# Seven products of half blocks for a SwiGLU's gate and up projections: a float32 decoder block on one core

## The chip, the core and the metric

The kernel runs on one core of a Trainium2 chip. The core has a matrix engine (PE, whose weight loads are shown apart as PEld), a vector engine (DVE), a scalar engine (ACT), a general engine (POOL) and a queue engine (SP) that here only issues transfers. They run side by side, each takes its own instructions in order, and they wait for one another by semaphores. The metric is the device time of one execution in microseconds (us); lower is better.

## The reference

One decoder layer for 512 positions of 1024 features: a half-step feed-forward, a mixing part with causal attention and a gated chunk mixer, and a second half-step feed-forward. Only the two feed-forwards are changed:

```python
D_MODEL = 1024; SEQ = 512; D_FF = 2816

def swiglu(h, w_gate, w_up, w_down):
    return (jax.nn.silu(h @ w_gate) * (h @ w_up)) @ w_down

x = x + 0.5 * swiglu(rms_norm(x, ffn1_norm[l]), ffn1_w_gate[l], ffn1_w_up[l], ffn1_w_down[l])
...
x = x + m @ w_out[l]
x = x + 0.5 * swiglu(rms_norm(x, ffn2_norm[l]), ffn2_w_gate[l], ffn2_w_up[l], ffn2_w_down[l])
```

## The kernel before

Activations lie feature-major: eight tiles of 128 features by 512 positions. A float32 product is made of three PE products of a rounded type: each operand is split into a rounded part (hi, a copy on ACT) and the rest (lo = source - hi, a subtraction on DVE), and `mm3` adds hi x hi, hi x lo and lo x hi in one bank of PSUM. PSUM has eight banks of 128x512, four under the name acc and four under att.

`ffn` is called twice (pools ff1 and ff2). It loops over 22 blocks `f` of 128 hidden features. For each, `dense` loads a 128x1024 chunk of gate weights and one of up weights, splits each, and runs 8 x 3 products for each chunk, 512 columns wide. `evacuate(f)` runs one block behind: DVE multiplies both banks by the row scale `r_bc` (L225, L228), ACT takes the SiLU, DVE multiplies (L229), and the result is split into `a_hi[f]`, `a_lo[f]`. After the last block comes the down projection: for each of 8 output tiles `j`, all 22 blocks are added in one bank, and `finish` adds half of it to the residual tile.

`prepare` names work put in after a block: in the first feed-forward the sum of squares and the scale after block 0 and the constants of the mixing part after block 8, in the second the scale after block 1. The raw weights have two buffers and the split weights three, so the queue loads and the splits run about two chunks ahead of PE. In the mixing part, `add_out` ends the stage before the second feed-forward: eight units of 24 products, each followed by the residual sum, `normed_input` (xg_hi on ACT, xg_lo on DVE) and `add_squares`.

A scheduler fixes the order of each engine's instructions when the program is built; the code's order is where it starts from.

Of the kernel before, what the change touches and what calls it, by code (L numbers as in the profile page):

```python
# [13 lines left out]
F32 = mybir.dt.float32  # L14
F32R = mybir.dt.float32r
# [5 lines left out]
P = 128  # L21
# [23 lines left out]
WARM = 8  # L45

# [10 lines left out]
def decoder_block(  # L57
# [85 lines left out]
    ones = const.tile([P, P], F32, name="ones")  # L143
# [3 lines left out]
    nc.vector.memset(ones, 1.0)  # L147
    nc.vector.memset(eps_col, NORM_EPS)
    ones_r = const.tile([P, P], F32R, name="ones_r")
    nc.vector.tensor_copy(ones_r, ones)  # L150
# [3 lines left out]
    for _ in range(WARM):  # L154
        nc.tensor.matmul(ps[:, :P], lhsT=ones, rhs=ones, start=True, stop=True)
# [18 lines left out]
    sq_sum = keep.tile([P, T], F32, name="sq_sum")  # L174
    x1_dram = [tc.dram_tile([P, T], F32, name=f"x1_dram{j}") for j in range(KD)]
# [28 lines left out]
    def dense(srcs, load=None):  # L204

        cuts = 1 if load is None else 4
        w = [chunk(src, cuts=cuts) for src in srcs]
        ps = [any_bank() for _ in srcs]
        for k in range(KD):
            s = slice(k * P, (k + 1) * P)  # L210
            if load is not None:
                load(k)
                if k % 2 == 0:
                    for c in w:
                        c[2](k // 2)
            for c, o in zip(w, ps):
                mm3(o, c[0][:, s], c[1][:, s], xg_hi[k], xg_lo[k], k == 0, k == KD - 1)
        return ps

    def ffn(pool, gu, dn, finish, load, prepare):  # L220
        a_hi, a_lo = [], []

        def evacuate(f, gate, up):
            g = scratch()
            nc.vector.tensor_tensor(g, gate, r_bc, op=ALU.mult)  # L225
            nc.scalar.activation(g, g, AF.Silu)
            u = scratch()
            nc.vector.tensor_tensor(u, up, r_bc, op=ALU.mult)  # L228
            nc.vector.tensor_tensor(u, u, g, op=ALU.mult)  # L229
            hi = pool.tile([P, T], F32R, name=f"a_hi{f}")  # L230
            lo = pool.tile([P, T], F32R, name=f"a_lo{f}")
            split(hi, lo, u)
            a_hi.append(hi)
            a_lo.append(lo)

        waiting = deque()
        for f in range(NF):
            if f == 0:
                banks = dense([gu[f, 0], gu[f, 1]], load)
            else:  # L240
                banks = dense([gu[f, 0]]) + dense([gu[f, 1]])
            waiting.append((f, *banks))
            if f in prepare:
                prepare[f]()
            if f > 0:
                evacuate(*waiting.popleft())
        evacuate(*waiting.popleft())
        for j in range(KD):
            ps = any_bank()
            for f0 in range(0, NF, 8):  # L250
                n = min(8, NF - f0)
                hi, lo = chunk(dn[j, :, f0 * P : (f0 + n) * P], n * P)
                for i in range(n):
                    s = slice(i * P, (i + 1) * P)
                    f = f0 + i
                    mm3(ps, hi[:, s], lo[:, s], a_hi[f], a_lo[f], f == 0, f == NF - 1)
            finish(j, ps)
# [73 lines left out]
    with tc.tile_pool(name="ff1", bufs=1) as ff1:  # L331
# [15 lines left out]
        def finish1(j, ps):  # L347
            nc.vector.scalar_tensor_tensor(xt[j], ps, 0.5, xt[j], op0=ALU.mult, op1=ALU.add)
            normed_input(j, xt[j], 1)
            add_squares(j, xt[j])  # L350
            nc.gpsimd.dma_start(out=x1_dram[j], in_=xt[j])

        ffn(ff1, gu1, dn1, finish1, load1, {0: prepare1, 8: constants1})


    x1 = []
# [541 lines left out]
```

## Time and profile before

| | |
|---|---|
| median of 3 runs | 1212.06 us (1212.02 to 1213.16) |
| the profiled execution's own time | 1214.09 us |
| its span, first to last instruction | 1212.4 us |
| PE busy | 99% of the span, 5322 products |
| DVE busy, ACT busy | 53%, 41% |
| granted PE clock, mean | 0.999 of full speed |
| bytes moved | 115.60 MB, 95 GB/s |

The page gives for each engine its busy time; the chain that ended last names, from the end backwards, what each step waited for. Three stages follow one another: the first feed-forward to about 415 us, the mixing part to about 838 us, and the second feed-forward. A share over the whole span mixes them, so the rows further down are read stage by stage.

### The profile page before, as it was taken

Reading aid. Unit: us, or ns where it says so; the run is one execution under the profiler, and the core shown is the slowest. Engines: PE = TensorE matmul, PEld = TensorE weight load, DVE = VectorE, ACT = ScalarE, POOL = GpSimd, SP = SyncE. Lnnn points to the kernel's source line nnn. Section 1 sums busy time; section 2 is a strip of 40 time slices with the busy share of each in tenths; the row PEclk is TensorE's granted clock in tenths of the full one; section 3 lists DMA queues with packets and bytes.
Section 4 is the critical chain, followed back from the end, with each engine's and each line's share of the span. In section 5 each row is a group of like instructions: output and inputs, shape, how many; then the busy total and the mean of one; then the engine's idle time right before and its main releaser. Section 6 shows DMA issues by size and latency. Waiting matters only on the chain.

```text
span 1212.4 us, 13634 instructions
## 1 busy us (share of the span) xinstructions
PE 1200.9 (99%) x5322; PEld 970.0 (80%) x5322; DVE 639.3 (53%) x1110; ACT 495.2 (41%) x756; POOL 24.1 (2%) x50
## 2 busy tenths in 40 slices
PE   8999999999999999999999999999999999999998
PEld 6888888888888888888878787888888888888886
DVE  5646444433333767876778876554543444442221
ACT  6324232222222554557587966233422323221110
POOL 0000000000000100000000000000000000000000
PEclk9999999999999999999999999999999999999999
DMA  5332322223333322222212124322323222233330
GB/s 176 104 109 87 98 94 93 98 78 113 113 113 122 127 91 87 70 87 71 70 53 87 35 74 153 104 87 87 104 87 105 87 93 98 90 98 113 113 112 31
DMA packets 34432, 115.60 MB, mean 95 GB/s; under 512 B 4032, under 2 KB 5088, under 8 KB 34368
## 3 DMA queue, kind: packets, MB, share of 16 engines
q1 hardware_dynamic: 32544, 109.07, 27.8%
q0 software_dynamic: 1824, 5.67, 1.5%
q8 instruction: 41, 0.67, 0.2%
q14 instruction: 23, 0.19, 0.0%
HBM read 110.53 MB, written 4.19 MB: 95 GB/s over the span
## 4 chain that ended last, share of the span: by engine, by line
PE 94%; ACT 3%; DVE 2%; DMA 0%; issue 0%; SPq 0%; DVEq 0%; ACTq 0%
PE bank_acc L125 16%; PE bank_acc L123 16%; PE bank_acc L124 16%; PE bank_att L124 10%; PE bank_att L125 10%; PE bank_att L123 10%; PE bank_acc L396 4%; PE bank_acc L395 4%; PE bank_acc L394 4%; PE bank_att L523 1%; PE bank_att L524 1%; PE bank_att L549 1%; DMA x<-in_x 0%; ACT scratch L531 0%; ACT w_hi L137 0%
## 5 line engine op out<-in xcount | busy, mean ns | idle before, releaser
L137 ACT CAST w_hi<-w_raw 128x1024 fp32r<-128x1024 f32 (+2 forms) x210 | 211.2, 1009 | 572.7 <-PE bank_acc L124 270.4
L138 DVE TENSOR_TENSOR w_lo<-w_raw,w_hi 128x1024 fp32r<-128x1024 f32 (+2 forms) x210 | 246.1, 1174 | 176.8 <-ACT w_hi L137 176.3
L123 PE MATMUL bank_acc<-xg_hi,w_hi 128*128 128x512 f32 x512 | 203.8, 398 | 2.5 <-ACT w_hi L137 1.5
L125 PE MATMUL bank_acc<-xg_hi,w_lo 128*128 128x512 f32 x512 | 203.5, 397 | 1.2 <-DVE w_lo L138 1.2
L124 PE MATMUL bank_acc<-xg_lo,w_hi 128*128 128x512 f32 x512 | 203.4, 397 | 0.1
L123 PE MATMUL bank_att<-xg_hi,w_hi 128*128 128x512 f32 x352 | 139.3, 396 | 0.0
L124 PE MATMUL bank_att<-xg_lo,w_hi 128*128 128x512 f32 x352 | 139.2, 396 | 0.0
L125 PE MATMUL bank_att<-xg_hi,w_lo 128*128 128x512 f32 x352 | 139.2, 395 | 0.0
L123 PEld LDWEIGHTS bank_acc<-xg_hi,w_hi 128*128 128x128 f32 x512 | 96.5, 188 | 26.3 <-ACT w_hi L137 2.3
L125 PEld LDWEIGHTS bank_acc<-xg_hi,w_lo 128*128 128x128 f32 x512 | 96.5, 188 | 24.6 <-DVE w_lo L138 1.6
L124 PEld LDWEIGHTS bank_acc<-xg_lo,w_hi 128*128 128x128 f32 x512 | 96.5, 188 | 23.0 <-DVE xg_lo L180 0.5
L228 DVE TENSOR_TENSOR scratch<-bank_att,r_bc 128x512 f32<-128x512 f32 x44 | 30.4, 691 | 132.3 <-PE bank_att L125 132.3
L394 PE MATMUL bank_acc<-w_hi,xg_hi 128*128 128x512 f32 x224 | 89.5, 400 | 0.0
L395 PE MATMUL bank_acc<-w_lo,xg_hi 128*128 128x512 f32 x224 | 88.7, 396 | 0.0
L396 PE MATMUL bank_acc<-w_hi,xg_lo 128*128 128x512 f32 x224 | 88.6, 396 | 0.0
L123 PEld LDWEIGHTS bank_att<-xg_hi,w_hi 128*128 128x128 f32 x352 | 66.1, 188 | 16.2
L125 PEld LDWEIGHTS bank_att<-xg_hi,w_lo 128*128 128x128 f32 x352 | 66.1, 188 | 15.9
L124 PEld LDWEIGHTS bank_att<-xg_lo,w_hi 128*128 128x128 f32 x352 | 66.1, 188 | 15.9
L225 DVE TENSOR_TENSOR scratch<-bank_acc,r_bc 128x512 f32<-128x512 f32 x44 | 30.4, 691 | 88.8 <-PE bank_acc L125 88.7
L125 PE MATMUL bank_att<-a_hi,w_lo 128*128 128x512 f32 x176 | 69.6, 396 | 0.0
L123 PE MATMUL bank_acc<-a_hi,w_hi 128*128 128x512 f32 x176 | 69.6, 396 | 0.0
L124 PE MATMUL bank_acc<-a_lo,w_hi 128*128 128x512 f32 x176 | 69.6, 396 | 0.0
(217 smaller groups left out, 1758.0 us busy)
## 6 DMA issues: line engine op xcount, KB each, us to landing
w_raw<-in_gu SPq DMA_DIRECT2D x86, 512.0 KB, 3.5
w_raw<-in_dn SPq DMA_DIRECT2D x32, 512.0 KB, 3.6
w_raw<-in_w_qk SPq DMA_DIRECT2D x16, 512.0 KB, 3.5
w_raw<-in_dn SPq DMA_DIRECT2D x16, 384.0 KB, 3.1
w_raw<-in_w_v SPq DMA_DIRECT2D x8, 512.0 KB, 3.4
w_raw<-in_w_ga SPq DMA_DIRECT2D x8, 512.0 KB, 3.4
w_raw<-in_w_gb SPq DMA_DIRECT2D x8, 512.0 KB, 3.5
w_raw<-in_w_pb SPq DMA_DIRECT2D x8, 512.0 KB, 3.5
```

What stands on the lines that cost most here:

```text
L123: nc.tensor.matmul(ps, lhsT=lhi, rhs=rhi, start=first, stop=False)
L124: nc.tensor.matmul(ps, lhsT=lhi, rhs=rlo, start=False, stop=False)
L125: nc.tensor.matmul(ps, lhsT=llo, rhs=rhi, start=False, stop=last)
L137: latest["hi"] = nc.scalar.copy(hi, src)
L138: latest["lo"] = nc.vector.tensor_tensor(lo, src, hi, op=ALU.subtract)
L225: nc.vector.tensor_tensor(g, gate, r_bc, op=ALU.mult)
L228: nc.vector.tensor_tensor(u, up, r_bc, op=ALU.mult)
L394: nc.tensor.matmul(banks[t], lhsT=xg_hi[k][:, ts], rhs=hi[:, s], start=k == 0, stop=False)
L395: nc.tensor.matmul(banks[t], lhsT=xg_hi[k][:, ts], rhs=lo[:, s], start=False, stop=False)
L396: nc.tensor.matmul(banks[t], lhsT=xg_lo[k][:, ts], rhs=hi[:, s], start=False, stop=k == KD - 1)
L523: nc.tensor.matmul(s[m], lhsT=qd[m][:, qs], rhs=kd[m][:, :w], start=True, stop=False)
L524: nc.tensor.matmul(s[m], lhsT=ql[m][:, qs], rhs=kd[m][:, :w], start=False, stop=False)
```

## The change

The gate and up projections now go by pairs of blocks (a "quad" `q`: two blocks `f`, gate and up, the lower and the upper half of the 1024 features, and the first and second 256 positions). The eight products of half blocks that the pair needs become seven, by sums of weight halves (`total`, made on DVE for each quad) and sums of activation halves (`half_sums`, made on DVE once for each feed-forward, split into `s_hi`, `s_lo`). Each product has 24 PE instructions 256 columns wide, in place of 512-wide ones. Three of the seven results share the bank `a` in turn, two share `c`; copies of partial results go to SBUF in between (`kept`, on ACT). In the first feed-forward quad 0 stays as it was, by full products (`first_quad`), and the half sums are made after it; in the second they are made before quad 0. The down projection runs in three groups (after blocks 0 to 7, 8 to 15, 16 to 21), with its sum kept in SBUF (`y`), and the scale of the up half is applied to that sum at the end. Raw weights get six buffers and split weights four. The residual tiles are read again from memory for the last addition, for which `add_out` now also writes them.

```diff
+    def half_sums(pool, norm):
+        s_hi, s_lo = [], []
+        def add(kt, x1, x2):
+            y = []
+            for j, xt in ((kt, x1), (kt + HK, x2)):
+                y.append(scratch())
+                g = gains[:, norm * KD + j : norm * KD + j + 1]
+                nc.vector.tensor_scalar(y[-1], xt, g, None, op0=ALU.mult)
+            f = pool.tile([P, 4, HT], F32, name="sums", tag="g", bufs=2)
+            (a11, a21), (a12, a22) = ((t[:, :HT], t[:, HT:]) for t in y)
+            nc.vector.tensor_tensor(f[:, 1], a11, a21, op=ALU.subtract)
+            nc.vector.tensor_tensor(f[:, 0], a22, a21, op=ALU.subtract)
+            nc.vector.scalar_tensor_tensor(f[:, 2], f[:, 0], -1.0, a11, op0=ALU.mult, op1=ALU.subtract)
+            nc.vector.scalar_tensor_tensor(f[:, 3], a12, -1.0, f[:, 2], op0=ALU.mult, op1=ALU.subtract)
...
+            split(s_hi[kt], s_lo[kt], f)
...
+        def quad(q):
+            b11, b12, b22, b21 = (raw_tile() for _ in range(4))
+            for i, t in enumerate((b11, b12, b22, b21)):
+                nc.sync.dma_start(out=t.rearrange("p (f c) -> p f c", f=2), in_=block(q, i))
+            def total(x, y):
+                t = pool.tile([P, 1024], F32, name="w_sum", tag="w_sum", bufs=2)
+                nc.vector.tensor_tensor(t, x, y, op=ALU.add)
+                return t
+            def product(ps, w, x, first=False):
+                hi, lo = parts()
+                split(hi, lo, w)
+                of = operand(x)
+                for f in range(2):
+                    o = ps[:, f * HT : (f + 1) * HT]
+                    for kt in range(HK):
+                        s = slice((f * HK + kt) * P, (f * HK + kt + 1) * P)
+                        x_hi, x_lo = of(kt)
+                        for i, (l, r) in enumerate(((hi, x_hi), (hi, x_lo), (lo, x_hi))):
+                            nc.tensor.matmul(
+                                o, lhsT=l[:, s], rhs=r, start=first and f == kt == i == 0,
+                                stop=kt == HK - 1 and i == 2, skip_group_check=True,
+                            )
+            def kept(ps):
+                t = scratch()
+                nc.scalar.copy(t, ps)
+                return t
+            two = dict(f=2)
+            g = pool.tile([P, 2, T], F32, name="g", tag="g", bufs=2)
+            a, c, e = bank(acc), bank(att), any_bank()
+            product(a, b11, "A11", True)
+            p1 = kept(a)
+            t3 = total(b12, b22)
+            product(c, t3, "S1", True)
+            p7 = kept(c)
+            t2 = total(t3, b11)
+            product(a, t2, "S2")
+            u2 = kept(a)
+            product(c, total(t2, b21), "A22")
...
+            product(a, total(b11, b12), "S0")
+            nc.vector.tensor_tensor(p7, a, p7, op=ALU.add)
+            product(e, b21, "A12", True)
...
+            nc.vector.tensor_tensor(g, g, r_bc.unsqueeze(1).to_broadcast([P, 2, T]), op=ALU.mult)
+            nc.scalar.activation(g, g, AF.Silu)
+            product(a, b22, "S3")
...
+            split(*activated(q), g)
...
+        for f0 in range(0, NF, 8):
+            n = min(8, NF - f0)
+            for q in range(f0 // 2, (f0 + n) // 2):
+                if q == 0 and load is not None:
+                    first_quad()
+                    for kt in range(HK):
+                        add_sums(kt, xt[kt], xt[kt + HK])
+                    continue
+                if q == 0:
+                    for kt in range(HK):
+                        add_sums(kt, xt[kt], xt[kt + HK])
+                quad(q)
+            for j in range(KD):
...
+                    mm3(ps, hi[:, s], lo[:, s], a_hi[f // 2][:, f % 2], a_lo[f // 2][:, f % 2], i == 0, i == n - 1)
+                if f0 == 0:
+                    y.append(residual.tile([P, T], F32, name=f"y_{j}", tag="x"))
+                    nc.scalar.copy(y[j], ps)
+                else:
+                    nc.vector.tensor_tensor(y[j], y[j], ps, op=ALU.add)
+                if f0 + n == NF:
+                    nc.vector.tensor_tensor(y[j], y[j], r_bc, op=ALU.mult)
+                    finish(j, y[j])
...
-        ffn(ff1, gu1, dn1, finish1, load1, {0: prepare1, 8: constants1})
+        ffn(ff1, gu1, dn1, 0, xt, finish1, load1, {0: prepare1, 5: constants1})
...
-        ffn(ff2, gu2, dn2, finish2, None, {1: norm_scale})
+        ffn(ff2, gu2, dn2, 2, x1, finish2, None, {0: norm_scale})
```

Three places show how the instructions stand. On DVE in the middle of a feed-forward, one block of before (scratch holds the scaled gate and up halves, w_lo the rest of a split weight chunk):

```order
L225 TENSOR_TENSOR scratch<-bank_acc,r_bc 128x512
L138 TENSOR_TENSOR w_lo<-w_raw,w_hi 128x1024
L228 TENSOR_TENSOR scratch<-bank_att,r_bc 128x512
L229 TENSOR_TENSOR scratch<-scratch 128x512
L138 TENSOR_TENSOR w_lo<-w_raw,w_hi 128x1024
L138 TENSOR_TENSOR a_lo_1065<-scratch,a_hi_1064 128x512
```

The same engine in a quad of the change, from the sum that follows product A22 (L342) to the two last multiplications (L356, L357):

```order
L342 TENSOR_TENSOR g<-bank_att,scratch 128x2x256
L140 TENSOR_TENSOR w_lo<-w_raw,w_hi 128x1024
L346 TENSOR_TENSOR scratch<-bank_acc,scratch 128x512
L140 TENSOR_TENSOR w_lo<-w_sum,w_hi 128x1024
L307 TENSOR_TENSOR w_sum<-w_sum,w_raw 128x1024
L348 TENSOR_TENSOR g<-bank_acc,scratch 128x2x256
L140 TENSOR_TENSOR w_lo<-w_sum,w_hi 128x1024
L353 TENSOR_TENSOR g<-g,r_bc 128x1024
L307 TENSOR_TENSOR w_sum<-w_raw 128x1024
L140 TENSOR_TENSOR w_lo<-w_sum,w_hi 128x1024
L356 TENSOR_TENSOR g<-bank_acc,g 128x2x256
L357 TENSOR_TENSOR g<-scratch,g 128x2x256
```

Weight sums (L307) now stand between the splits and the reads of PSUM; the splits there belong to products of the next quad, up to four products ahead.

On DVE at the start of the second feed-forward, before, from the last residual sum of the mixing part (x_7) on:

```order
L734 TENSOR_TENSOR x_7_6209<-x_7_6209,bank_acc 128x512
L138 TENSOR_TENSOR w_lo<-w_raw,w_hi 128x1024
L180 SCALAR_TENSOR_TENSOR xg_lo_118<-x_7_6209,gains,xg_hi_110 128x512
L188 TENSOR_TENSOR sq_sum<-sq_sum,scratch 128x512
L138 TENSOR_TENSOR sq_lo<-sq_sum,sq_hi 128x512
L138 TENSOR_TENSOR w_lo<-w_raw,w_hi 128x1024 x4
```

And in the change, the same place:

```order
L869 TENSOR_TENSOR x_7_7238<-x_7_7238,bank_acc 128x512
L218 TENSOR_SCALAR scratch<-x_0_7224,gains 128x512
L181 SCALAR_TENSOR_TENSOR xg_lo_116<-x_7_7238,gains,xg_hi_108 128x512
L189 TENSOR_TENSOR sq_sum<-sq_sum,scratch 128x512
L218 TENSOR_SCALAR scratch<-x_4_7232,gains 128x512
L221 TENSOR_TENSOR sums<-scratch 128x256
L222 TENSOR_TENSOR sums<-scratch 128x256
L218 TENSOR_SCALAR scratch<-x_1_7226,gains 128x512
L223 SCALAR_TENSOR_TENSOR sums<-sums,scratch 128x256
L218 TENSOR_SCALAR scratch<-x_5_7234,gains 128x512
L224 SCALAR_TENSOR_TENSOR sums<-scratch,sums 128x256
```

All half sums (tiles 0 to 3, of x_0 with x_4 and so on) stand behind the last residual sum; the rest of the fourth, s_lo for tile 3, is the 34th row from x_7's on.

On PE at the same place, before, from the last product of the mixing part on:

```order
L125 MATMUL bank_acc<-m_hi_6503,w_lo 128x512
L123 MATMUL bank_acc<-xg_hi_103,w_hi 128x512
L124 MATMUL bank_acc<-xg_lo_111,w_hi 128x512
L125 MATMUL bank_acc<-xg_hi_103,w_lo 128x512
L123 MATMUL bank_att<-xg_hi_103,w_hi 128x512
```

In the change, from the last of the 24 instructions of quad 0's first product (A11) on:

```order
L320 MATMUL bank_acc<-xg_hi_104,w_lo 128x256
L320 MATMUL bank_att<-s_hi_7846,w_hi 128x256
L320 MATMUL bank_att<-s_lo_7847,w_hi 128x256
L320 MATMUL bank_att<-s_hi_7846,w_lo 128x256
L320 MATMUL bank_att<-s_hi_7859,w_hi 128x256
L320 MATMUL bank_att<-s_lo_7860,w_hi 128x256
L320 MATMUL bank_att<-s_hi_7859,w_lo 128x256
L320 MATMUL bank_att<-s_hi_7872,w_hi 128x256
L320 MATMUL bank_att<-s_lo_7873,w_hi 128x256
L320 MATMUL bank_att<-s_hi_7872,w_lo 128x256
L320 MATMUL bank_att<-s_hi_7885,w_hi 128x256
```

The second product reads the half sums of all four tiles, and follows the first directly.

## Rows read from the trace of the kernel before

**Rows 1.** The page: busy time of the engines; shares of the chain that ended last.
```profile
PE 1200.9 (99%) x5322; PEld 970.0 (80%) x5322; DVE 639.3 (53%) x1110; ACT 495.2 (41%) x756; POOL 24.1 (2%) x50
...
PE 94%; ACT 3%; DVE 2%; DMA 0%; issue 0%; SPq 0%; DVEq 0%; ACTq 0%
```
**Rows 2.** Waits of PE, longest first: total us, times, longest.
```profile
PE bank_acc L123 <- ACT w_hi L137: 1.5, 2, 0.8
```
**Rows 3.** Busy time by stretch, with counts; then PE clock, DMA share, GB/s.
```profile
100.00:200.00 100.00, 100.00 (x430) 80.54 (x429) 48.31 (x79) 31.89 (x40) 0.00 (x0) 1.00 0.28 93
```
**Rows 4.** Products in order of time (start, us each), gated mixer; a load-queue instruction.
```profile
491.36 0.28 PE L671 MATMUL bank_att<-ws_lo,va_hi 128*128 128x256 f32 x1
...
492.54 0.28 PE L672 MATMUL bank_att<-ws_hi,va_lo 128*128 128x256 f32 x1
492.66 0.40 PE L523 MATMUL bank_att<-k,q 128*128 128x512 f32 x1
...
L670 PEldq EVENT_SEMAPHORE  x5: 51/51/51, 477.4 to 495.7; - x5
```
**Rows 5.** Groups by shape: busy us, mean ns of one, idle before.
```profile
L138 DVE TENSOR_TENSOR w_lo<-w_raw,w_hi 128x1024 fp32r<-128x1024 f32 x186 | 227.8, 1225 | 176.8 <-ACT w_hi L137 176.3
L225 DVE TENSOR_TENSOR scratch<-bank_acc,r_bc 128x512 f32<-128x512 f32 x44 | 30.4, 691 | 88.8 <-PE bank_acc L125 88.7
L138 DVE TENSOR_TENSOR w_lo<-w_raw,w_hi 128x256 fp32r<-128x256 f32 x8 | 3.0, 419 | 0.0
L620 DVE TENSOR_SCALAR scratch<-scratch,mv,ln_rs 128x512 f32<-128x512 f32 x4 | 2.2, 539 | 0.0
L137 ACT CAST w_hi<-w_raw 128x1024 fp32r<-128x1024 f32 x186 | 195.1, 1050 | 520.8 <-PE bank_acc L124 245.3 <-issue 153.7 <-PE bank_att L124 79.8
L226 ACT ACTIVATE scratch<-scratch 128x512 f32<-128x512 f32 x44 | 27.5, 627 | 2.3 <-DVE scratch L225 2.3
```
**Rows 6.** DVE in order of time where it waits for nothing: start, us each.
```profile
31.17 1.22 DVE L138 TENSOR_TENSOR w_lo<-w_raw,w_hi 128x1024 fp32r<-128x1024 f32 x1
32.31 0.69 DVE L160 SCALAR_TENSOR_TENSOR r_bc<-scratch,r_bc 128x512 f32<-128x512 f32 x1
33.03 0.69 DVE L225 TENSOR_TENSOR scratch<-bank_acc,r_bc 128x512 f32<-128x512 f32 x1
33.63 0.68 DVE L228 TENSOR_TENSOR scratch<-bank_att,r_bc 128x512 f32<-128x512 f32 x1
```
**Rows 7.** Transfers by kind: count, KB each, median us from issue to landing.
```profile
w_raw<-in_gu SPq DMA_DIRECT2D x86, 512.0 KB, 3.5
```
**Rows 8.** The first feed-forward's start: ACT's scale; PE's last product of block 1.
```profile
29.17 0.63 ACT L201 ACTIVATE r_bc<-scratch 128x512 f32<-128x512 f32 x1
...
34.14 0.40 PE L125 MATMUL bank_att<-xg_hi,w_lo 128*128 128x512 f32 x1
```
**Rows 9.** The second feed-forward's start: last residual sum; a stretch as in rows 3.
```profile
838.29 0.69 DVE L734 TENSOR_TENSOR x<-x,bank_acc 128x512 f32<-128x512 f32 x1 [2.22 <-PE bank_acc L125]
...
838.00:850.00 12.00, 12.00 (x54) 9.64 (x53) 4.19 (x6) 4.21 (x6) 0.00 (x0) 1.00 0.14 46
```
**Rows 10.** Two stretches in block 1 of the first feed-forward, as in rows 3.
```profile
18.50:22.00 3.50, 1.62 (x6) 0.73 (x5) 3.29 (x6) 1.99 (x3) 0.00 (x0) 1.00 0.02 6
22.00:25.50 3.50, 3.50 (x11) 2.66 (x10) 1.80 (x3) 0.62 (x1) 0.00 (x0) 0.53 0.72 195
```
**Rows 11.** Two stretches, without and with the mixing part's constants, as in rows 3.
```profile
86.00:97.00 11.00, 11.00 (x49) 8.87 (x48) 4.90 (x6) 3.06 (x5) 0.00 (x0) 1.00 0.29 95
97.00:108.00 11.00, 11.00 (x49) 8.86 (x48) 9.61 (x47) 6.28 (x10) 0.00 (x0) 1.00 0.28 93
```
**Rows 12.** The end in order of time: last product, last sum, issue of the output.
```profile
1207.91 0.40 PE L125 MATMUL bank_att<-a_hi,w_lo 128*128 128x512 f32 x1
...
1208.34 0.69 DVE L813 SCALAR_TENSOR_TENSOR x<-bank_att,x 128x512 f32<-128x512 f32 x1 [13.81 <-PE bank_att L125]
1209.06 0.34 SPq L814 DMA_DIRECT2D out_x<-x  x1
```

More of the change, by code (lines that the diff above doesn't have):

```diff
@@ L146, in decoder_block @@
     make_identity(nc, ident)
-    nc.vector.memset(ones, 1.0)
+    ones_r = const.tile([P, P], F32R, name="ones_r")
+    nc.vector.memset(ones_r.bitcast(F32), 1.0)
     nc.vector.memset(eps_col, NORM_EPS)
-    ones_r = const.tile([P, P], F32R, name="ones_r")
-    nc.vector.tensor_copy(ones_r, ones)
     ready = const.tile([P, 1], F32, name="ready")
@@ L154, in decoder_block @@
     for _ in range(WARM):
-        nc.tensor.matmul(ps[:, :P], lhsT=ones, rhs=ones, start=True, stop=True)
+        nc.tensor.matmul(ps[:, :P], lhsT=ones_r.bitcast(F32), rhs=ones_r.bitcast(F32), start=True, stop=True)
     def rsqrt_newton(y, v, t):
@@ L174, in decoder_block @@
     sq_sum = keep.tile([P, T], F32, name="sq_sum")
+    x2_dram = [tc.dram_tile([P, T], F32, name=f"x2_dram{j}") for j in range(KD)]
     x1_dram = [tc.dram_tile([P, T], F32, name=f"x1_dram{j}") for j in range(KD)]
@@ L202, in norm_scale @@
         rsqrt_newton(r_bc, v, t)
[L204 to L225, printed above, removed]
-            nc.scalar.activation(g, g, AF.Silu)
[L227 to L252, printed above, removed]
@@ new lines, in half_sums, with operand, of @@
+    def half_sums(pool, norm):
[12 more added lines that the diff above has]
+            nc.vector.scalar_tensor_tensor(f[:, 3], a12, -1.0, f[:, 2], op0=ALU.mult, op1=ALU.subtract)
+            s_hi.append(pool.tile([P, 4, HT], F32R, name=f"s_hi{kt}"))
+            s_lo.append(pool.tile([P, 4, HT], F32R, name=f"s_lo{kt}"))
+            split(s_hi[kt], s_lo[kt], f)
+        def operand(name):
+            def of(kt):
+                if name[0] == "A":
+                    j, ts = kt + HK * (name[2] == "2"), slice(HT * (name[1] == "2"), HT * (name[1] == "2") + HT)
+                    return xg_hi[j][:, ts], xg_lo[j][:, ts]
+                i = int(name[1])
+                return s_hi[kt][:, i], s_lo[kt][:, i]
+            return of
+        return add, operand
@@ L736, in evacuate @@
                 add_squares(n, xr)
+                nc.gpsimd.dma_start(out=x2_dram[n], in_=xr)
             add_feature_major(w_o[n], m_hi, m_lo, evacuate)
```

92 lines of the change are left out of this document (80 added, 12 removed).

## Prediction

> **What bounds the kernel now.** I read the page first, then PE's waits, then single stretches. PE is busy 99% of the span and makes up 94% of the chain that ended last [rows 1]; its longest entry of waiting is 1.5 us in all [rows 2]. So before asking what DVE or ACT does, the reader should ask what PE's instructions cost. In a feed-forward 430 of the 512-wide products start in 100 us, 0.2325 us each, at full clock, and DVE is busy 48 of the 100 us [rows 3]. Busy times of PE say nothing here (one product is shown as 0.40 us, and they overlap), so I go by starts. DVE has half its time free in these stages, and the change spends that half.
>
> **The products.** A pair of blocks takes 2 x 48 = 96 wide products, 96 x 0.2325 = 22.32 us. In the change it takes 7 x 24 = 168 products of 256 columns. The trace has such products with a new weight load each in the gated mixer: 11 of them start between 491.36 and 492.66 us, 0.1182 us each [rows 4]. A quad is then 168 x 0.1182 = 19.86 us, 2.46 us less. Ten quads of the first feed-forward and eleven of the second gain 21 x 2.46 = **51.7 us**. The down projections keep their 2 x 528 wide products. The weak point is that the run in the trace is short, and the gain is the difference of large numbers: each ns on the narrow product costs 3528 x 1 ns = 3.5 us. An instruction on the load queue that only waits took 51 ns [rows 4]; two of that kind fit into 0.118 us, but that is no proof for hundreds in a row.
>
> **DVE in a quad.** Seven splits, four weight sums, one scaling and one activation split are 13 instructions of 128x1024; five read PSUM or combine 128x512. As durations [rows 5] that is 13 x 1.225 + 5 x 0.691 = 19.4 us. Where DVE waits for nothing, though, a 1024-wide one starts 1.14 us ahead of the next and a 512-wide one 0.60 us [rows 6], so 13 x 1.14 + 5 x 0.60 = 17.8 us. Both ends lie under 19.86 us; I take 17.8 with a little waiting, since most neighbours in the order are independent.
>
> The Trainium skill (VectorE: DVE Perf Modes, "The DRAIN you can't avoid") speaks against this: the next operation can't start until the pipe is empty, though the page itself lets one that is not held start earlier. The rows differ from the first statement (0.60 us between starts of 0.69 us operations). By the strict reading the quads still fit, but the half sums below would take 34 x 0.085 = 2.9 us longer at each start and the kernel 1202 us, an estimate with that page.
>
> Does the order let DVE use its time? I walked one quad by hand through the order with the durations of rows 5. Splits run up to four products ahead (four buffers), and a buffer comes free when PE ends the product four earlier. With t = 0 at the start of A11, the sum after A22 runs at 12.3 (A22 ends at 11.35), the one after S0 at 14.3 to 15.0, and S3, which overwrites its bank, starts at 17.0; the split of S0 is done at 6.2 and needed at 11.35. So DVE may fall about 2 us behind before PE waits, and it regains 1 to 2 us in each quad. ACT needs 8 x 1.05 for splits, 1.1 for SiLU and 3 x 0.63 for copies, 11.4 us [rows 5]: not the bound. The weight sum t3 waits for a raw tile whose buffer comes free some 3.8 us earlier on DVE; a chunk lands 3.5 us after its issue [rows 7], so that wait is 0 to 1 us in a quad and DVE's free time covers it; if that were gone, 21 x 1 us. In quad 5 the constants of the mixing part come on top: 9.61 - 4.90 = 4.7 us on DVE [rows 11], so it ends up to 2.6 us late there. Price 0 to 2.6, taken **1.0**.
>
> **The start of each feed-forward** is what the half sums cost, since product S1 needs all four tiles of them and only A11 (24 x 0.1182 = 2.84 us) lies ahead of it on PE. In the second feed-forward none of it can start early by the order: all half sums stand behind the residual sum of x_7, which starts at 838.29 us, when PE has just ended the mixing part [rows 9]. From there to the last s_lo DVE has 34 instructions: three 512-wide of x_7 (0.75 + 0.65 + 0.65), 8 scalings (0.539 - 0.085 = 0.45 each), 8 differences of 256 (0.419 - 0.085 = 0.33), 8 combined ones (0.37, between the last two), 4 s_lo, 2 weight sums and a w_lo (1.14 each): 2.05 + 3.6 + 2.7 + 3.0 + 8.0 = 19.3, with waits for ACT 19.6 us. Then 14 products of S1 are left, 1.65 us: S1 ends 21.3 us after the stage began, where unhindered it would at 5.68. PE waits **15.6 us**; before, it had no gap there (12.00 of 12.00 us, [rows 9]).
>
> In the first feed-forward the sums come after ACT's scale, which ended at 29.8 us [rows 8]. Its matmuls now stand about 1 to 3 us earlier, so I start at 28. DVE has the same 31 instructions of half sums and weight sums (17.3 us), the scale's own three (1.9), four reads of quad 0's banks (2.4) and its split (1.14): 22.7 us, with waits s_lo is done at 51.0 and S1 at 52.7. Without a wait it would be 34.37 (block 1's end before, [rows 8]) + 5.68 = 40.05. Net **12.5 us**; 11.6 to 14.3 as the start moves.
>
> PE is idle more than 10 us in each, and the clock falls after idleness: in block 1 before, a stretch with PE busy 1.6 of 3.5 us is followed by one at 0.53 of full clock, which is the 1.2 GHz level, with 11 products started instead of 15 [rows 10]. Four products are 0.9 us there; the half-speed part runs over S1's last 14 instructions and what follows. I take 1.7 us at each start, **3.4** in all, between 1.8 and 7.
>
> **Smaller terms.** Before a down group, the last quad's a_lo is done 3.8 to 4.2 us after S3: ACT 1.05, DVE 0.69 twice and 1.225, more where a w_lo stands between. PE has 18 products (4.19 us) of earlier blocks to do in the groups of eight, 12 (2.80 us) in the group of six: 0.8 us late there, twice, **1.6**; 0 to 5. The sums into `y` and the second reads of the residual lie beside PE's 4.2 to 5.6 us for each `j`. At the end two DVE steps are added between the last product and the output's issue, which today follow 0.43 + 0.72 us apart [rows 12]: 2 x 0.72 = **1.4**.
>
> **Sum.** -51.7 + 12.5 + 15.6 + 3.4 + 1.6 + 1.0 + 1.4 = **-16.2 us**. The profiled execution would go from 1214.09 to 1197.9 (span 1212.4 to 1196.2); the median, 2.0 us lower than that execution, from 1212.06 to **1196 us**. A gain of 51.7 us, then, of which the half sums give two thirds back.
>
> **Rivals.**
> *DVE becomes the bound in the quads* (the other side). Place: the splits and PSUM reads of each quad. If each of the 18 instructions takes its full duration and 0.1 us of waiting, DVE needs 19.4 + 1.8 = 21.2 us, and PE waits for it: 21 x (21.2 - 19.86) = 28 us, 1224 us. It decides from 19.86 + 16.2/21 = 20.6 us for a quad. For it: DVE is in order and its reads of PSUM hold the splits behind them. Against it: rows 6.
> *Narrow products don't hold 0.118 us in a long run.* The gain is gone at 0.1182 + 16.2/3528 = 0.1228 us. At 0.124, 5% more, 1216 us. For it: the run in rows 4 is 11 long and follows wide products, in whose time instructions could be queued. Against it: no slowing within the run. The Trainium skill (TensorE: Matmul & The Clock Gate, "Wait — 56ns, not 53.3ns?") gives about 62 ns of sequencer time for a matmul with one way of decoding; if a weight load costs as much, a pair needs 124 ns, an estimate from that page that no run here shows yet.
> *The starts cost half*: single-source scalings and sums that run faster than the nearest rows, or sums that overlap more. 14 us less, 1182 us. Nothing in the trace speaks for it.
> *Small waits in every quad*, 0.5 us, from hand-overs that my walk leaves out: 21 x 0.5 = 10, 1206 us.
>
> **Chances.** Forecast, 1188 to 1204: 0.58. Small waits, 1204 to 1210: 0.12. DVE-bound, 1212 to 1226: 0.12. Slow narrow products: 0.08. Cheaper starts: 0.10. A measurement of this kernel can tell about 0.2% (2.4 us) from no change. Faster by more: 0.58 + 0.12 + 0.10 - 0.01 = 0.79; the edge between the cases, within 0.2%: 0.05; slower: 0.16. The range from 1182 to 1216 leaves out most of the DVE-bound case, half of the slow products and the lowest cheap starts, together under 0.2. The forecast's own range is 1188 to 1204.
>
> **What the profile after would show.** Products: 168 starts in 19.9 us in the middle of a feed-forward, DVE busy about 95%. Start of the second feed-forward: after 24 narrow products PE idle some 13 us until DVE's first w_lo of a weight sum, then a stretch near half clock. First feed-forward: the same at about 36 to 49 us. If PE's gaps are spread over all quads, ended by DVE, the walk was wrong; if starts are 0.124 us apart without gaps, the price of the narrow product was; if PE has no gap at the two starts, the order of the half sums was misread.

## The result and the profile after

The changed kernel takes **1196.7 us** (median of 4 runs, 1195.15 to 1197.43) beside 1212.61 us of the kernel before (1212.02 to 1213.84): ratio 0.9866, 95% interval 0.9849 to 0.9883. The profiled execution took 1197.43 us, with a span of 1195.6. The forecast was 1196 us and a span of 1196.2. The total is right; two of its parts are not, and they cancel.

The page, with the lines that answer to [rows 1], and PE's clock by 40 slices of 29.9 us:

```profile
PE 1156.7 (97%) x6834; PEld 1017.2 (85%) x6834; DVE 868.6 (73%) x1342; ACT 600.5 (50%) x869; POOL 37.1 (3%) x74
PEclk9799999999999999999999999999799999999999
PE 89%; DVE 4%; ACT 3%; DMA 2%; issue 1%; POOL 0%; POOLq 0%; DVEq 0%; ACTq 0%
```

PE is still the bound, but it now has idle stretches, and two dips of the clock show where: slice 2 and slice 29. The waits of PE (total us, times, longest), to be read against [rows 2]:

```profile
PE bank_att L320 <- ACT w_hi L139: 21.7, 2, 12.0
PE bank_att L194 <- ACT sq_hi L139: 4.9, 1, 4.9
PE bank_att L320 <- DVE w_lo L140: 1.5, 2, 0.7
```

The first entry is the two starts, which were forecast. The second, the scale ahead of the mixing part, was not. Stretches, to be read against [rows 3] and [rows 9]: the four quads of a group, then the second feed-forward's start (busy time of PE, PEld, DVE, ACT, POOL with counts, clock, DMA share, GB/s):

```profile
149.97:169.90 19.93, 19.93 (x169) 19.92 (x168) 14.47 (x14) 9.28 (x11) 1.18 (x3) 1.00 0.31 98
169.90:189.80 19.90, 19.90 (x171) 19.90 (x170) 19.35 (x42) 13.57 (x15) 0.55 (x1) 1.00 0.38 114
189.80:209.72 19.92, 19.92 (x171) 19.92 (x169) 19.89 (x36) 12.14 (x15) 0.00 (x0) 1.00 0.35 107
209.72:229.64 19.92, 19.92 (x171) 19.92 (x169) 16.00 (x17) 11.47 (x13) 0.00 (x0) 1.00 0.50 159
834.60:846.90 12.30, 0.27 (x4) 0.07 (x2) 12.30 (x27) 4.67 (x5) 0.00 (x0) 0.59 0.44 166
846.90:850.90 4.00, 2.83 (x10) 2.24 (x10) 4.00 (x5) 2.10 (x2) 0.00 (x0) 0.50 0.00 0
850.90:856.80 5.90, 5.86 (x38) 5.86 (x39) 4.79 (x6) 2.68 (x3) 0.00 (x0) 0.75 0.08 3
```

A quad takes 19.92 us with no gap. At the start PE is idle for 12.0 of 12.3 us while DVE is busy for all of them, and then runs at 0.50 of full clock, the 1.2 GHz level. The last stretch holds the second half of S1 and all of S2, 38 products: from 851.32 us on the trace has 12 of them 0.2125 us apart without a wait, and the rest 0.119 us apart. In order of time, the first and last instruction of the half sums in the first feed-forward, then the second's start with PE's two around the gap:

```profile
26.51 0.48 DVE L218 TENSOR_SCALAR scratch<-x,gains 128x512 f32<-128x512 f32 x1
46.66 1.22 DVE L140 TENSOR_TENSOR s_lo<-sums,s_hi 128x1024 fp32r<-128x1024 f32 x1
...
832.03 0.69 DVE L869 TENSOR_TENSOR x<-x,bank_acc 128x512 f32<-128x512 f32 x1 [2.77 <-PE bank_acc L127]
832.63 0.48 DVE L218 TENSOR_SCALAR scratch<-x,gains 128x512 f32<-128x512 f32 x1
834.55 0.27 PE L320 MATMUL bank_acc<-xg_hi,w_lo 128*128 128x256 f32 x1
835.17 0.42 DVE L221 TENSOR_TENSOR sums<-scratch 128x256 f32<-128x256 f32 x1
835.51 0.42 DVE L222 TENSOR_TENSOR sums<-scratch 128x256 f32<-128x256 f32 x1
846.86 0.58 PE L320 MATMUL bank_att<-s_hi,w_hi 128*128 128x256 f32 x1 [12.03 <-ACT w_hi L139]
849.79 1.22 DVE L140 TENSOR_TENSOR s_lo<-sums,s_hi 128x1024 fp32r<-128x1024 f32 x1
```

The stage sums, from the starts of the first and last products of each stage in the two traces (a product's pitch of 0.23 us added to the last):

| us | before | after | change |
|---|---|---|---|
| first feed-forward, to its last product | 381.57 | 367.49 | -14.1 |
| from there to the end of the scale's products (48 others between) | 11.66 | 17.57 | +5.9 |
| mixing part, to its last product | 444.86 | 446.76 | +1.9 |
| second feed-forward | 370.05 | 358.54 | -11.5 |
| from its last product to the end | 4.24 | 5.27 | +1.0 |

The second row is the part that was left out. Its rows, end of the first feed-forward: POOL writes `y` (L486), reads `x` for a later tile (L482), and DVE (L483) waits for the read.

```profile
365.13 0.54 POOL L486 DMA_DIRECT2D x_dram<-y  x1 [4.62 <-DVE y L483]
365.66 0.54 POOL L482 DMA_DIRECT2D scratch<-in_x  x1
369.06 0.69 DVE L483 SCALAR_TENSOR_TENSOR y<-y,scratch 128x512 f32<-128x512 f32 x1 [0.76 <-DMA scratch<-in_x]
370.05 0.54 POOL L486 DMA_DIRECT2D x_dram<-y  x1 [3.84 <-DVE y L483]
370.58 0.54 POOL L482 DMA_DIRECT2D scratch<-in_x  x1
383.75 0.79 PE L194 MATMUL bank_att<-sq_hi,ones_r 128*128 128x512 f32 x1 [4.90 <-ACT sq_hi L139]
385.06 0.63 PE L529 MATMUL bank_acc<-w_hi,xg_hi 128*128 128x512 f32 x1
385.49 0.63 PE L530 MATMUL bank_acc<-w_lo,xg_hi 128*128 128x512 f32 x1
```

Each write waits for the tile's sum, the sum for its read, and the read stands on POOL behind the write of the tile before: a loop of 4.9 us between these two tiles and up to 6.1 between others, against PE's 18 x 0.2325 = 4.2 us. Most of the 5.9 us is PE's idle stretch of 4.9 us that is shown above; the rest goes with the scale's two products, which run at half clock. The end of the kernel, to be read against [rows 12]:

```profile
1190.13 0.40 PE L127 MATMUL bank_acc<-a_hi,w_lo 128*128 128x512 f32 x1
1190.57 0.69 DVE L387 TENSOR_TENSOR y<-y,bank_acc 128x512 f32<-128x512 f32 x1 [2.06 <-PE bank_acc L127]
1191.29 0.69 DVE L389 TENSOR_TENSOR y<-y,r_bc 128x512 f32<-128x512 f32 x1
1192.02 0.69 DVE L950 SCALAR_TENSOR_TENSOR y<-y,scratch 128x512 f32<-128x512 f32 x1
1192.73 0.33 SPq L951 DMA_DIRECT2D out_x<-y  x1
```

### The profile page after: what moved, and what is told of

Its sections match the earlier page's. It is cut to its first block, busy times and chain, and to the rows that moved or that the text cites. A ratio compares the mean times of both kernels' runs of the same rounds, so it can differ in the third digit from the quotient of the medians.

```text
span 1195.6 us, 17191 instructions
## 1 busy us (share of the span) xinstructions
PE 1156.7 (97%) x6834; PEld 1017.2 (85%) x6834; DVE 868.6 (73%) x1342; ACT 600.5 (50%) x869; POOL 37.1 (3%) x74
## 4 chain that ended last, share of the span: by engine, by line
PE 89%; DVE 4%; ACT 3%; DMA 2%; issue 1%; POOL 0%; POOLq 0%; DVEq 0%; ACTq 0%
PE bank_acc L320 22%; PE bank_att L320 12%; PE bank_acc L125 10%; PE bank_acc L126 9%; PE bank_acc L127 9%; PE bank_acc L530 4%; PE bank_acc L531 4%; PE bank_acc L529 4%; PE bank_att L126 4%; PE bank_att L127 4%; PE bank_att L125 4%; DMA scratch<-in_x 1%; PE bank_att L658 1%; PE bank_att L659 1%; PE bank_att L684 1%
## 5 line engine op out<-in xcount | busy, mean ns | idle before, releaser
L139 ACT CAST w_hi<-w_raw 128x1024 fp32r<-128x1024 f32 (+2 forms) x195 | 189.5, 979 | 273.7 <-PE bank_acc L126 93.2
L320 PE MATMUL bank_acc<-s_hi,w_hi 128*128 128x256 f32 x504 | 142.4, 283 | 0.9 <-ACT w_hi L139 0.9
L320 PE MATMUL bank_acc<-s_lo,w_hi 128*128 128x256 f32 x504 | 142.0, 282 | 0.0
L320 PE MATMUL bank_acc<-s_hi,w_lo 128*128 128x256 f32 x504 | 141.8, 281 | 0.0
L140 DVE TENSOR_TENSOR w_lo<-w_sum,w_hi 128x1024 fp32r<-128x1024 f32 x84 | 102.3, 1219 | 28.5 <-ACT w_hi L139 28.5
L320 PEld LDWEIGHTS bank_acc<-s_hi,w_hi 128*128 128x128 f32 x504 | 95.6, 190 | 1.6 <-ACT w_hi L139 1.5
L320 PEld LDWEIGHTS bank_acc<-s_lo,w_hi 128*128 128x128 f32 x504 | 95.4, 189 | 0.0
L320 PEld LDWEIGHTS bank_acc<-s_hi,w_lo 128*128 128x128 f32 x504 | 95.4, 189 | 0.0
L125 PE MATMUL bank_acc<-xg_hi,w_hi 128*128 128x512 f32 x176 | 70.8, 402 | 1.1 <-ACT w_hi L139 1.1
L127 PE MATMUL bank_acc<-xg_hi,w_lo 128*128 128x512 f32 x176 | 70.4, 400 | 0.0
L126 PE MATMUL bank_acc<-xg_lo,w_hi 128*128 128x512 f32 x176 | 70.3, 399 | 0.0
L320 PE MATMUL bank_att<-xg_hi,w_hi 128*128 128x256 f32 x248 | 69.7, 281 | 0.0
```

What stands on the lines that cost most here:

```text
L125: nc.tensor.matmul(ps, lhsT=lhi, rhs=rhi, start=first, stop=False)
L126: nc.tensor.matmul(ps, lhsT=lhi, rhs=rlo, start=False, stop=False)
L127: nc.tensor.matmul(ps, lhsT=llo, rhs=rhi, start=False, stop=last)
L139: latest["hi"] = nc.scalar.copy(hi, src)
L140: latest["lo"] = nc.vector.tensor_tensor(lo, src, hi, op=ALU.subtract)
L320: nc.tensor.matmul(o, lhsT=l[:, s], rhs=r, start=first and f == kt == i == 0, stop=kt == HK - 1 and i == 2, skip_group_check=True,)
```

## The experiments

Each one edits the changed kernel. Its ratio is to the kernel before in the same session (the change itself: 0.9866, 0.9849 to 0.9883).

**The reads of the residual.**

```diff
+        reload(j + 2)
-            xr = scratch()
-            nc.gpsimd.dma_start(out=xr, in_=x[:, j, :])
+            xr = again.pop(j)
```

> Edit: in the last down group of the first feed-forward the reads of x on POOL are issued two output tiles ahead, so that none stands behind the write of the tile before it. Theory (reads serialised behind the writes make each output tile last 5 to 6 us against PE's 4.2): the idle stretch of PE before the next stage's scale, 5.3 us, and the half-clock stretch after it, about 2.4 us, go; 5 to 8 us less than 1196.7, so 1189 to 1192, and the waits of DVE for the tile read from x (8.8 us, 6 times) are under 2 us. Rival (DVE's own six instructions for an output tile, about 4.2 us, are as slow): 1194 or more, and the idle stretch stays above 3 us, ended by the same scale, with DVE busy through it.

Measured: 1189.8 us, ratio 0.981 (0.9796 to 0.9823). The scale's products end 11.66 us after the first feed-forward, as before the change, and the mixing part takes 444.85 us, as before; DVE waits for no read of x any more. The theory stands, and DVE's own instructions, the rival, are not what was slow. It splits the cost: 5.9 us up to the end of the scale, and 1.9 us of products at half clock behind it.

**Cover at the starts: one narrow product more.**

```diff
             product(a, b11, "A11", True)
             p1 = kept(a)
+            if q in ahead:
+                product(e, b21, "A12", True)
```

> Edit: in the first quad by seven products of each feed-forward, product A12, which needs no half sums, stands ahead of S1. Theory (PE lacks work that needs no half sums while DVE makes them): S1 starts when it did, A12's 2.84 us move into the wait, and each start costs 2.84 us less: about 5.7 us less than 1196.7, 1191, with idle stretches of about 7 and 9.5 us in place of 9.95 and 12.3. Rival (the split of A12 delays the chain of half sums on DVE by 1.14 us, or the clock falls just as far): 1193 to 1196.

Measured: 1191.86 us, 0.9828 (0.9815 to 0.9842). The first down groups begin 2.5 and 2.1 us earlier, less than the 2.84 us each. That is about the theory's number, but not quite its mechanism: A12's own split stands on DVE behind most of the half sums, so PE now waits at A12 (8.4 us idle at the first start, 3.8 + 7.1 at the second), and in the first feed-forward S1 starts at 47.6 us, not at 43.7 as in the change. A22 begins at 54.1 us in both: what DVE needs does not shrink, PE only does more beside it.

**Cover by a whole wide quad.**

```diff
+                if q == (load is not None):
+                    wide_quad(q)
+                    for kt in range(HK):
+                        add_sums(kt, xt[kt], xt[kt + HK])
+                    continue
```

> Edit: the first quad by seven products of each feed-forward goes by full 512-wide products instead (the second quad of the first feed-forward, the first of the second), and the half sums are made beside it. Theory (the two starts cost 11.3 and 16.5 us only because three narrow products are too little cover): both idle stretches go, two quads lose 2.4 us each, so about 23 us less than 1196.7: 1174, or up to 1178 if waits of 1 to 2 us stay. Rival (DVE lacks the time, not PE the cover: DVE has 13 to 17 us of half sums and weight sums, and some 10 us of the wide quad's own, for 22.3 us): waits of 4 us or more stay at each start, 1182 to 1188.

Measured: 1200.04 us, 0.9891 (0.9877 to 0.9904), about 3 us slower than the change. Neither range holds. In the first feed-forward the half sums began beside the wide quad, but the last of them ended only at 64.1 us, since weight sums and splits stand between them, and S1 waits for them; its first down group begins at 101.49 us, 4.0 us earlier than the change's. In the second feed-forward, which starts at 825.86 us here, they did not run beside the wide quad at all, and the first down group begins 105.05 us after the stage's start in place of 96.61. DVE comes to them only here, behind the scale's L158, which in the program now stands ahead of them:

```profile
851.73 0.69 DVE L158 SCALAR_TENSOR_TENSOR scratch<-r_bc 128x512 f32<-128x512 f32 x1
852.34 0.48 DVE L218 TENSOR_SCALAR scratch<-x,gains 128x512 f32<-128x512 f32 x1
```

DVE was busy for only 13.61 of the 22.30 us of that wide quad. The run settles little about cover, and shows that the place in the program decides.

**Half sums product by product.** S1's four differences first, then those of S2, S0 and S3, and the order A11, A12, S1, A22, S2, S0, S3:

```diff
+                product(a, b11, "A11", True)
+                product(e, b21, "A12", True)
+                first(xt)
...
+                product(c, t3, "S1", True)
+                product(c, total(t2, b21), "A22")
+                others(xt)
+                product(a, t2, "S2")
```

> Edit: in the same two quads the order is A11, A12, S1, A22, S2, S0, A later S3, and the half sums are made product by product instead of tile by tile: S1's differences first, straight from the residual tiles with the gain in the split, then those of S2, S0 and S3. Seven products as before, some 2 us less on DVE. Theory (what is late is S1's operand, which has to wait for sums that only later products need): S1 starts about 3 us after A12 in the first and 2 us after in the second feed-forward, S2 waits 4 to 5 us more; 12 to 16 us less than 1196.7, 1181 to 1185. Rival (DVE's total is what binds in the 20 us from the start, in whatever order): 3 to 6 us less, 1191 to 1194, as with A12 alone.

Measured: 1190.09 us, 0.9812 (0.9799 to 0.9826): 6.6 us less than the change, half of what the theory wanted and just past the rival's. S1 does start early, but in the first feed-forward PE stops 2.5 us at S2, and in the second it stops 4.0 us ahead of S1, at A12, whose weights landed late:

```profile
833.67 1.05 ACT L139 CAST w_hi<-w_raw 128x1024 fp32r<-128x1024 f32 x1 [0.38 <-DMA w_raw<-in_gu]
```

**Half sums off DVE.** ACT scales, POOL subtracts:

```diff
-            nc.vector.tensor_tensor(f[:, 1], a11, a21, op=ALU.subtract)
+            nc.gpsimd.tensor_tensor(f[:, 1], a11, a21, op=ALU.subtract)
```

> Edit: the half sums leave DVE: ACT makes the scaled copies, POOL the 16 differences of 256 columns for each feed-forward, DVE keeps only the four s_lo. Order of the first narrow quad: A11, A12, S1, A22, S2, S0, S3, and A12's weights are loaded second. Theory (the start costs what DVE has too much to do there: about 13 us of half sums on top of quads with some 2 us free each, so order and cover alone give little back, as seen): 8.8 us less of DVE at each start; what is left is the delay to the last difference, 3 to 4 us behind A12; 15 to 22 us less than 1196.7, 1175 to 1182, if POOL takes about 0.5 us for a difference. Rival (POOL is slow, over 1 us for each, or holds DVE up): S1 starts no earlier than with A12 alone, 1188 to 1195.

Measured: 1206.15 us, 0.995 (0.9937 to 0.9964), 9 us slower than the change and beyond the rival's range too; S1's waits grew from 9.95 and 12.3 to 15.3 and 17.3 us. Both halves of the rival are in the trace, in order of time:

```profile
26.45 0.69 DVE L160 SCALAR_TENSOR_TENSOR scratch<-r_bc 128x512 f32<-128x512 f32 x1 [0.29 <-ACT r_bc L204]
28.19 1.23 DVE L161 TENSOR_TENSOR scratch<-scratch 128x512 f32<-128x512 f32 x1
28.83 1.19 POOL L226 TENSOR_TENSOR sums<-scratch 128x256 f32<-128x256 f32 x1
37.95 0.72 POOL L225 TENSOR_TENSOR sums<-scratch 128x256 f32<-128x256 f32 x1 [5.08 <-DVE s_lo L140]
38.20 1.55 DVE L140 TENSOR_TENSOR a_lo<-g,a_hi 128x1024 fp32r<-128x1024 f32 x1 [0.34 <-ACT a_hi L139]
38.63 1.70 POOL L226 TENSOR_TENSOR sums<-scratch 128x256 f32<-128x256 f32 x1
40.41 0.72 POOL L227 TENSOR_TENSOR sums<-scratch,sums 128x256 f32<-128x256 f32 x1
```

A difference of 128x256 takes POOL 0.72 us alone (the last row), against DVE's 0.42 ([rows 5]). Where it runs beside a DVE instruction, one of the two mostly grows: POOL's took 1.1 to 1.8 us in 12 cases, and where POOL's began first, at 37.95 us, it kept its 0.72 us and DVE's split took 1.55 us in place of 1.22. DVE's 512-wide instruction took 1.23 us in place of 0.69 twice. (POOL also waits for the two buffers of `sums`, the 5.08 us above.) The Trainium skill (Perfetto Trace Analysis, "Optimizing Scalar/DVE Operations") warns that GpSimd and DVE share a read port, so that moving work between these two may not help. The rows agree.

**A wide quad, with the half sums ahead of it.**

```diff
+                    for kt in range(HK):
+                        add_sums(kt, xt[kt], xt[kt + HK])
                     wide_quad(q)
-                    for kt in range(HK):
-                        add_sums(kt, xt[kt], xt[kt + HK])
```

> Edit: as with the wide cover, a full quad of 512-wide products in each feed-forward beside the half sums, but the half sums stand ahead of it in the program, so that DVE begins them at once and not behind the scale that follows the wide quad. Theory (DVE's work up to the end of the first group of quads sets the time: 9.8 us for a wide quad, 13.4 of half sums, 3 x 17.8, 78.5 us in the second feed-forward, for 82 us of PE): the first down group of the second feed-forward starts 83 to 87 us after the stage in place of 96.6, that of the first at 99 to 102 us; 12 to 17 us less than 1196.7, 1180 to 1185. Rival (something other than DVE's order and amount, such as the late landing of the first weights, holds S1): the second stage's first group stays above 92 us, 1190 or more.

Measured: 1170.67 us, 0.9653 (0.964 to 0.9666), 26 us less than the change, where 12 to 17 were expected. The second feed-forward's first down group starts 84.2 us after the stage, as expected; the first feed-forward's at 93.2 us, 6 us better than the best expected. Reckoned from the run with all quads wide (98.07 and 89.47 us, further down) less 2.33 us for each narrow quad, a start without any wait would give 93.4 and 82.5 us: the first start's loss is gone, and 1.7 us of the second's is left. The wide quad and the narrow one behind it, first and second feed-forward:

```profile
31.00:53.40 22.40, 22.40 (x99) 18.14 (x98) 22.18 (x35) 10.86 (x13) 0.00 (x0) 1.00 0.18 55
53.40:73.30 19.90, 19.90 (x170) 19.90 (x169) 18.06 (x18) 10.78 (x12) 0.00 (x0) 1.00 0.32 106
817.20:839.50 22.30, 20.83 (x91) 16.65 (x90) 21.48 (x37) 10.09 (x11) 0.54 (x1) 1.00 0.46 154
839.50:859.40 19.90, 19.90 (x160) 19.46 (x159) 19.43 (x23) 14.48 (x17) 0.00 (x0) 1.00 0.34 106
```

DVE is almost as busy as in the change's gaps, but PE has 22.3 us of work beside it that needs no sum, and its clock stays at 1.00. The loss at the starts can be covered, if the sums stand at the right place. Two things change at once here: PE gets work, and DVE has some 8 us less to do (the expectation's 9.8 us for a wide quad, 17.8 for a narrow one). How much each gave is not shown; cover with no less work for DVE, A12 alone, gave less than 5 us.

**The clock at the starts.** PE runs products that nobody reads while it waits:

```diff
+            if q == (load is not None):
+                idle = any_bank()
+                for _ in range(40 if load else 50):
+                    nc.tensor.matmul(idle, lhsT=xg_hi[0][:, :P], rhs=xg_hi[0], start=True, stop=True)
```

> Edit: PE does products that nobody reads while it waits for S1's operand: 40 of 512 columns after A11 in the first feed-forward's first narrow quad (about 9.3 of 9.95 us), 50 in the second's (11.6 of 12.3 us). Everything else as in the change. Theory A (the fall of the clock is a cost of its own, S2 takes 5.9 to 6.3 us at half clock in place of 2.84): S1 and S2 run at full clock and 6 us or more go, 1190 to 1191. Theory B (behind the half sums, DVE's splits of S2, A22 and S0 set the pace, so the half clock hides behind them): S1 and S2 run at full clock but wait in between for DVE, and only 1 to 3 us go, 1194 to 1196.

Measured: 1197.53 us, 0.9877 (0.9863 to 0.989), not to be told from the change and above both theories. The second feed-forward's start, in the stretches that are shown above for the change:

```profile
834.60:846.90 12.30, 11.73 (x54) 9.43 (x52) 12.30 (x26) 4.60 (x5) 0.00 (x0) 1.00 0.46 170
846.90:850.90 4.00, 1.98 (x10) 1.37 (x10) 4.00 (x6) 2.02 (x3) 0.00 (x0) 0.92 0.00 0
850.90:856.80 5.90, 5.68 (x26) 5.69 (x27) 4.90 (x5) 2.76 (x4) 0.00 (x0) 0.50 0.00 0
```

S1 begins at nearly full clock, but DVE hands over its tiles no sooner; PE waits again, and now the rest of S1 and half of S2 run at the lower level. Theory A's 6 us are not there, and could not be: it took the 5.9 us stretch for S2 at half clock, but that stretch holds half of S1 too, and only a dozen of its 38 products ran slowly. The change's own trace says what the half clock costs there: behind the last half sum PE no longer waits, and 17 products in the first feed-forward and 12 in the second start 0.21 us apart in place of 0.119, an estimate of 1.6 and 1.1 us.

**Room on DVE in the quads.** Two of the four weight sums of every quad made twice, then all four:

```diff
+                for _ in range(2 if y is b21 or y is b12 else 1):
                     nc.vector.tensor_tensor(t, x, y, op=ALU.add)
```

> Edit: in every narrow quad two of the four weight sums on DVE are made twice (2 x 1.14 us of DVE more in a quad, 21 quads), with the same result. Theory (a quad has 17.4 to 17.8 us of DVE work for 19.9 us of PE, so about 2.2 us are free): 1196 to 1201, no idle stretches in the quads beyond those of the two starts. Rival (DVE, shown 19.4 to 19.9 us busy in the second and third quad of a group, is at its limit): 21 x 2.28 = 48 us less what the down groups give back, 1215 or more.

> Edit: all four weight sums of every narrow quad are made twice (4.56 us of DVE more in a quad). Theory (the limit lies at 19.9 us): DVE needs 22.0 us, PE waits 2.1 us in a quad except for the lead of about 2 us with which each of six groups begins; 44 less up to 12, so 1228 to 1242. Rival (more of DVE is free than its busy share shows, since most of its instructions overlap): under 1215.

Measured: 1210.79 us, 0.9985 (0.9976 to 0.9994), and 1241.63 us, 1.0237 (1.0223 to 1.0251). The second is at the top of its range. The first lies between theory and rival, and the starts of its quads say why: of 14.7 us more in the six groups of quads, 6.9 fall in the second feed-forward's first group, behind the half sums, 4.6 in the group with the mixing constants, 0.7 to 1.4 in three others and none in the last. So an undisturbed quad has the 2.2 us of room that was worked out; behind the second feed-forward's half sums and behind the constants it is already spent. Why the three quads behind the first feed-forward's half sums lose only 1.4 us is not shown.

**The products undone.** Every quad by 96 wide products, the rest of the change as it is:

```diff
-            product(a, b11, "A11", True)
...
+                    for k in range(KD):
+                        s = slice(k * P, (k + 1) * P)
+                        mm3(ps[e], hi[:, s], lo[:, s], xg_hi[k], xg_lo[k], k == 0, k == KD - 1)
```

> Edit: only the products are undone: every quad goes by 96 full products of 512 columns without sums of weights or activations; the three down groups, the sum in SBUF, the second reads of the residual and the buffers stay. Theory (the change is 21 quads at 19.9 us in place of 22.32, -50.6 us, the two starts +27.7 us, and the stage between and the end +9 us, of which the last two stay): 1196.7 + 50.6 - 27.7 = 1219.6, 1216 to 1222, with the idle stretch of 5 us at the end of the first feed-forward. Rival (three groups and the reads cost nothing of their own): 1209 to 1213.

Measured: 1214.09 us, 1.0014 (1.0005 to 1.0023), between the two ranges. Where this run's first down group, its second group of quads and the down group after that begin, and then where the change's first down group begins:

```profile
98.07 0.39 PE L125 MATMUL bank_acc<-a_hi,w_hi 128*128 128x512 f32 x1
142.56 0.39 PE L125 MATMUL bank_acc<-xg_hi,w_hi 128*128 128x512 f32 x1
231.55 0.39 PE L125 MATMUL bank_acc<-a_hi,w_hi 128*128 128x512 f32 x1
...
105.46 0.39 PE L125 MATMUL bank_att<-a_hi,w_hi 128*128 128x512 f32 x1
```

Four wide quads take 88.99 us here, 22.25 each, so the products give 21 x (22.25 - 19.92) = 48.9 us. The starts take most of it back: this run's first down group begins at 98.07 us, so three narrow quads without a wait would allow 98.07 - 3 x 2.33 = 91.1 in place of the change's 105.46, 14.4 us; in the second feed-forward 89.47 - 4 x 2.33 = 80.1 after the stage's start in place of 96.61, 16.5 us. With the wait for the reads, 2.7 us shorter here, the spans add up: 48.9 - 30.9 - 2.7 = 15.3, and 1211.0 - 1195.6 = 15.4. (The medians differ by 17.4 us; 2 us of that are not in this pair of profiles.) The theory was 5.5 us too high because it took the starts against the first blocks of before, which end 3.3 us later than the changed code's, the products at 22.32 us, and the wait for the reads as unchanged. The rival's reason, a change that costs nothing but its products, fails by the same wait: 15.8 us to the end of the scale, not 11.66.

**Both repairs together.** The wide quads, and the scale and residual added after the second group:

```diff
+                elif f0 + n < NF:
+                    nc.vector.tensor_tensor(y[j], y[j], ps, op=ALU.add)
+                    nc.vector.tensor_tensor(y[j], y[j], r_bc, op=ALU.mult)
+                    add_input(j, y[j])
+                else:
+                    t = scratch()
+                    nc.vector.scalar_tensor_tensor(t, ps, -0.5, r_bc, op0=ALU.mult, op1=ALU.mult)
+                    nc.vector.tensor_tensor(y[j], y[j], t, op=ALU.add)
```

> Edit: the wide quads with the half sums first, and besides this the scale and the residual are added to the sum in SBUF after the second down group, so that the last group's result needs two DVE steps in place of three and no read of x or x2 stands in the last group. Theory (the stage after the first feed-forward loses 5.9 us to the reads behind the writes and 1.9 us to the half clock, the end one DVE step of 0.6 us): 8 us less than 1170.7, 1161 to 1164, and the scale ends 11.7 to 12 us after the first feed-forward in place of 17. Rival (the 16 steps more of DVE in the second group, or the reads there, delay the quads of the last group): 1166 or more.

Measured: **1164.63 us**, ratio 0.9604 (0.9591 to 0.9617), faster than both kernels. The scale ends 11.66 us after the first feed-forward, the end takes 4.56 us in place of 5.27. That is 6.0 us less than the wide cover alone, not 8: there the mixing part had taken 444.86 us, so the 1.9 us of half clock were already gone, and the stage up to the end of the scale 17.10 us, so 5.4 us were left to gain.

## Why the prediction was right, point by point

**Products.** 51.7 us forecast, 48.9 to 50.4 measured (21 quads at 19.92 us, beside 22.25 or 22.32). The short run of [rows 4] held over 168 products: 0.1186 us each. The slow-products rival is out. The Trainium skill's sequencer time (TensorE: Matmul & The Clock Gate, "Wait — 56ns, not 53.3ns?"), counted once for the load and once for the matmul, would have been 124 ns a pair, an estimate that the trace does not bear out.

**DVE in a quad.** 17.8 us forecast. Four quads in a row have 69.7 us of it, 17.4 each with the constants in one of them; the four in the middle of the second feed-forward, without constants, have 66.5, 16.6 each. So the term was a little too high. The forecast of 95% busy was reached only in the middle two of the first four, with 97% and 100%; without constants the middle two are at 92%. The DVE-bound rival did not come true, and the two added sums show that its edge was near. The 1.0 us for the constants did not appear (that quad took 19.9 us), nor did small waits.

**The starts.** The mechanism, its place and about its size were right. In the second feed-forward the last s_lo ended 19.0 us after x_7's sum began (19.6 forecast), and with the clock 16.5 us were lost (15.6 + 1.7 forecast). The clock's share was 1.6 us in the first and 1.1 in the second, an estimate from the starts of the slow products, beside 1.7 each. In the first, reckoned from before's end of block 1 as the forecast did, it was 11.3 us up to A22 against 12.5 + 1.7: DVE began with the scale at 25.9 us, not 28, and the last s_lo was done at 47.9, not 51.0. (The forecast's own 52.7 - 40.05 is 12.65, not 12.5, which changes nothing.) The differences of 256 columns followed each other in 0.33 us, as [rows 5] and [rows 6] had it, and not as the strict reading of the Trainium skill's VectorE page has it (VectorE: DVE Perf Modes, "The DRAIN you can't avoid").

**Smaller terms.** The 1.6 us at the groups' boundaries did not appear: the group of six starts 0.12 us behind the last narrow product. The tail grew by 1.0 us, not 1.4: the two DVE steps did cost their 1.4 (2.60 us from the last product's start to the output's issue, 1.15 before), but the span ended 2.9 us after the issue in place of 3.3.

**What was missing.** The step "the second reads of the residual lie beside PE's 4.2 to 5.6 us for each `j`" failed. It looked at the length of a read and not at its place on POOL, behind a write that waits for the tile before. The price was 5.9 us up to the end of the scale and 1.9 us of half clock behind it, and the reads issued ahead gave back just that in these two stretches, 6.9 us in the whole kernel. By stage the forecast had been -24.6 + 12.5 + 1.7 + 0.8 + 1.0 = -8.6 us for the first feed-forward and -27.1 + 15.6 + 1.7 + 0.8 = -9.0 for the second; they gave -14.1 and -11.5. So the total hit because 7.8 us that were not foreseen stood against 5.5 and 2.5 us of costs priced too high. That it came within 1 us is luck; without the missed step the kernel takes 1189.8 us, still inside the range but near its lower end.

## What to carry to other kernels

When a change trades work of the bounding engine for work of another, look at the one-off part at the start of each stage: here it ate 30.9 of 48.9 us, and one pair of blocks of each stage left in the old form, with the sums ahead of it in the program, brought the first down groups 24.6 us forward. For a transfer, ask what it stands behind on its queue, above all when that is a write that waits for the transfer's own consumer. A free share of an engine is spent where its work bunches, and a run with that work doubled shows where.

## What the runs showed of the hardware

POOL and DVE hold each other up: 0.72 us for POOL's 128x256 difference alone, 1.1 to 1.8 where DVE was at work first, and DVE's 128x512 instruction at 1.23 in place of 0.69 us. Where DVE's instruction read one operand from PSUM, a difference beside it took 0.73 us, as alone (two cases). An idle stretch of PE costs more than its length: after 4.9 us of idleness the next products started 0.43 us apart in place of 0.2325 for 5.6 us, 2.9 us in all. And keeping PE busy up to the hand-over did not keep the clock up: after 4 us in which PE was busy for 2.0, it ran at 0.50.
